# Second layer's weight split: the low part's tile starts from minus the raw tile instead of minus the high part

## The chip, the cores and the metric

The kernel runs on one NeuronCore of a Trainium2 chip. The metric is the device time of one execution in microseconds (us), the median over runs. Six names of engines occur: PE is TensorE (matrix products), ACT is ScalarE, DVE is VectorE, POOL is GpSimd, SP is SyncE, which here only issues transfers, and DMA is the transfer engines.

## The reference

One inference step of a decoder trunk of two layers, over 512 prompt tokens and 8 x 8 sample tokens (576 columns), model width 1024. The first layer is a gated linear recurrence (HGRN2); behind it one shared K/V is made, and the second layer is attention over a window of 128 positions with a sink per head, with 32 heads and an inner width of 2048:

```python
q, gate = swa_in(hp, w_in_b[j], norm_b[j])        # rms_norm(x) @ w_in, split into q and gate
hp = swa_out(hp, swa_prompt(q, kv_p, sinks_b[j]), gate, w_out_b[j])
...
def swa_out(x, o, gate, w_out):
    return x + (o.astype(F32) * jax.nn.silu(gate.astype(F32))).astype(x.dtype) @ w_out
...
y_prompt = rms_norm(hp, norm_f)
```

All of it is in fp32. Only the weights `w_in_b` (1024 x 4096) and `w_out_b` (2048 x 1024) of the second layer are touched by the change.

## The kernel before

PE takes its operands here in a rounded form of fp32 (fp32r). To keep the accuracy, each operand is split into a high part (the rounded value) and a low part (what the rounding left), and a product is made of three: high by high, high by low, low by high. `product_cols` issues them in just that order: first all `whi` by the high part of the data, then `whi` by its low part, and last `wlo` by the high part. So a weight's low part is wanted a good two thirds into its first product.

The weights come in blocks of 128 x 1024 through `split_weights`. SP issues the load of the raw block (L198), into one of three `raw` buffers. In the second layer (`share[0]` is None) the low part is not made by a subtraction on DVE or POOL, as in the first layer, but by a DMA: ACT casts the high part (L201), ACT writes minus the high part into the low tile (L202), and POOL issues a DMA that adds the raw block onto the low tile (L203). `whi` and `wlo` have two buffers each. A raw buffer is free again when its cast and its DMA are done, and only then can SP's next load into it start.

There are 48 such blocks: 16 `bq` (queries, `queries`), 16 `bg` (gates, `gates`), 14 `o` (output products, `out_halves`), and 2 last `o` blocks of `out_last`, whose parts are not `whi`/`wlo` but pieces of `xhi`/`xlo` (the split activations, no longer needed by then). The work is written as generators, and `merged` weaves the attention's steps with the parts of a string ORDER that ends in "q6 g6 q7 g7 O4 o6". Behind the last, `o6`, `out_last` makes the final product (`pz`), and then the final norm follows. The program is then scheduled by the framework: within an engine, instructions are put in an order by readiness and priority as it estimates them, and each engine works its own list in that order. So the order in the source isn't always the order on an engine.

Other names that occur below: `ohb`/`olb` are high and low parts of the gated attention output (cast at L1399 and L1271 on ACT, subtraction at L1400 on DVE), the data of the `po` products. `P`, `st`, `ph`, `pk`, `pav`, `low` belong to the attention's softmax and its product with V. `Qs` and `QS` are the queries, copied from the `pbq` products for sample and prompt tokens, and `scs` is the product of the sample queries with the cached keys.

Of the kernel before, what the change touches and what calls it, by code (L numbers as in the profile page):

```python
# [10 lines left out]
F32 = mybir.dt.float32  # L11
# [4 lines left out]
AF = mybir.ActivationFunctionType  # L16
ALU = mybir.AluOpType
# [66 lines left out]
def yoco_kernel(  # L84
# [26 lines left out]
    act, dve, pool, pe, sp = nc.scalar, nc.vector, nc.gpsimd, nc.tensor, nc.sync  # L111
# [83 lines left out]
    def split_weights(src, name, parts=None):  # L195
        n = src.shape[1] * src.shape[2]
        raw = wts.tile([P, 1024], F32, tag="raw", name=f"raw_{name}", bufs=3)
        sp.dma_start(raw[:, :n].rearrange("p (a c) -> p a c", a=src.shape[1]), src)  # L198
        hi, lo = parts or [wts.tile([P, 1024], F32R, tag=t, name=f"{t}_{name}") for t in ("whi", "wlo")]
        if share[0] is None:  # L200
            act.copy(hi[:, :n], raw[:, :n])  # L201
            act.activation(lo[:, :n], hi[:, :n].bitcast(F32), AF.Copy, scale=-1.0)  # L202
            pool.dma_start(lo[:, :n].bitcast(F32), raw[:, :n], accum_op=ALU.add)  # L203
            return hi, lo
        act.copy(hi[:, :n], raw[:, :n])  # L205
        c = n * share[0] // 8
        for eng, r in ((dve, slice(0, c)), (pool, slice(c, n))):
            if r.start < r.stop:
                eng.tensor_tensor(lo[:, r], raw[:, r], hi[:, r].bitcast(F32), ALU.subtract)  # L209
        return hi, lo  # L210
# [209 lines left out]
    def out_product(w_out, k0, ogs):  # L420

        nk = len(ogs)
        wd = 256 if nk > 2 else 512
        for mc in range(D // wd):
            src = w_out[0, k0 * P : (k0 + nk) * P, mc * wd : (mc + 1) * wd].rearrange("(k p) c -> p k c", p=P)
            whi, wlo = split_weights(src, f"o{k0}_{mc}")
            for c in range(wd // P):
                m = mc * (wd // P) + c
                pm = main(f"po{k0}_{m}")
                for _ in product(  # L430
                    pm,
                    whi,
                    wlo,
                    lambda k, j: ogs[k][0][:, j * HN : (j + 1) * HN],
                    lambda k, j: ogs[k][1][:, j * HN : (j + 1) * HN],
                    width=wd,
                    c0=c * P,
                    nk=nk,
                ):
                    pass  # L440
                h2 = s2(hT[:, m, :])
                with early():
                    dve.tensor_add(h2, h2, ps2(pm))  # L443
                yield

    def out_scaled(w_out, k0, ogs, gname, one):
# [4 lines left out]
        for mc in range(D // wd):  # L451
            src = w_out[0, k0 * P : (k0 + nk) * P, mc * wd : (mc + 1) * wd].rearrange("(k p) c -> p k c", p=P)
            whi, wlo = split_weights(src, f"o{k0}_{mc}")
            for c in range(wd // P):
                m = mc * (wd // P) + c
                pm = main(f"po{k0}_{m}")
                for _ in product(
                    pm,
                    whi,
                    wlo,  # L460
                    lambda k, j: ogs[k][0][:, j * HN : (j + 1) * HN],
                    lambda k, j: ogs[k][1][:, j * HN : (j + 1) * HN],
                    width=wd,
                    c0=c * P,
                    nk=nk,
                ):
                    pass
                h2 = hT[:, m, :]
                with tc.high_priority(offset=BOOST):
                    dve.tensor_add(s2(h2), s2(h2), ps2(pm))  # L470
                    act.activation(xhi[:, m, :], h2, AF.Copy, scale=vec(gname, m))
                    dve.scalar_tensor_tensor(
                        xlo[:, m, :], h2, vec(gname, m), xhi[:, m, :].bitcast(F32), ALU.mult, ALU.subtract
                    )
                    if m == 0:
                        act.activation(rall, h2, AF.Square)
                    else:
                        sq = one(f"nsq{m}")
                        act.activation(sq, h2, AF.Square)
                        (pool if m in SUM_POOL else dve).tensor_tensor(rall, rall, sq, ALU.add)  # L480

    def out_last(w_out, k0, ogs, each, between):


        nk = len(ogs)
        wd = 1024 // nk
        ws = []
        for mc in range(nk):
            src = w_out[0, k0 * P : (k0 + nk) * P, mc * wd : (mc + 1) * wd].rearrange("(k p) c -> p k c", p=P)
            parts = [view(x, [[1, 1024]], off=1024 * mc) for x in (xhi[:, 0, :], xlo[:, 0, :])]  # L490
            ws.append(split_weights(src, f"o{k0}_{mc}", parts))
        for j in range(2):
            for m in range(KT):
                pm = half(f"pz{k0}_{j}_{m}")
                product_half(pm, *ws[m * P // wd], lambda k: ogs[k], j, wd, m * P % wd, nk)
                h1 = hT[:, m, j * HN : (j + 1) * HN]
                with tc.high_priority(offset=BOOST):
                    dve.tensor_add(h1, h1, pm[:, :HN])
                    each(j, m)
                between(j, m)  # L500
# [30 lines left out]
    with ExitStack() as actx:  # L531
# [430 lines left out]
        for h in range(NH):  # L962
            nxt, chunks, n = {}, [], 0
# [21 lines left out]
    with ExitStack() as bctx:  # L985
# [34 lines left out]
        with tc.tile_pool(name="kvx", bufs=1) as kvx:  # L1020
# [24 lines left out]
            for c in range(4):  # L1045
# [17 lines left out]
                else:  # L1063
# [5 lines left out]
                    hi = Vc[:, :, g0 : g0 + 2, :64]  # L1069
# [508 lines left out]
```

## Time and profile before

| what | value |
|---|---|
| median of 3 runs | 1154.66 us (1153.55 to 1154.71) |
| profiled execution, its own time | 1152.44 us |
| its span in the trace | 1150.6 us |
| PE busy | 1105.9 us, 96% of the span |
| DVE busy | 857.6 us, 75% |
| ACT busy | 749.4 us, 65% |
| POOL busy | 265.9 us, 23% |
| mean granted clock of PE | 0.987 |

The span is the time from the first to the last instruction on the core; the profiled execution's own time holds 1.84 us beside it. All times of day below are microseconds from the start of the span. The second layer takes it from about 717 us on.

### The profile page before, as it was taken

What the parts mean: (1) busy time and instruction counts of PE and PEld (TensorE: products, weight loads), DVE (VectorE), ACT (ScalarE), POOL (GpSimd) and SP (SyncE); (2) the same over time, 40 slices, a digit from 0 to 9 for tenths busy, and PEclk for the clock granted to TensorE, in tenths of its full rate; (3) what the DMA queues carried; (4) which work ended last, traced back from release to release, by engine and by line L of the source; (5) the groups of instructions that cost most, each with busy time, mean ns of one, the idle gap of its engine ahead of it and who ended that gap; (6) DMA issues with size and microseconds to landing.
All of it is one profiled execution on the core that took longest, in us unless ns stands there. A gap on an engine that the chain in (4) does not pass through costs nothing.

```text
span 1150.6 us, 27472 instructions
## 1 busy us (share of the span) xinstructions
PE 1105.9 (96%) x10937; PEld 1072.6 (93%) x10937; DVE 857.6 (75%) x2090; ACT 749.4 (65%) x1748; POOL 265.9 (23%) x311
## 2 busy tenths in 40 slices
PE   5999999999999999999999989899999999999997
PEld 4999999998999899999999979899999998999996
DVE  8897777399985498875597887666676767576676
ACT  6677765367673467773566655678866876777665
POOL 1122221021221032121122143332332242232220
PEclk7999999999999999999999999999999999999998
DMA  5332333223233433323323223655545555554552
GB/s 157 93 113 78 104 94 113 77 79 108 71 118 107 122 87 110 89 76 107 96 71 110 86 77 92 143 137 117 132 114 126 129 128 134 126 127 113 127 111 83
DMA packets 168010, 123.19 MB, mean 107 GB/s; under 512 B 4665, under 2 KB 158314, under 8 KB 167850
## 3 DMA queue, kind: packets, MB, share of 16 engines
q1 hardware_dynamic: 160970, 96.26, 28.4%
q0 software_dynamic: 6912, 25.17, 11.6%
q8 instruction: 86, 1.41, 0.5%
q14 instruction: 42, 0.34, 0.1%
HBM read 84.06 MB, written 14.16 MB: 85 GB/s over the span
## 4 chain that ended last, share of the span: by engine, by line
PE 51%; DVE 6%; ACT 3%; issue 1%; DMA 1%; POOL 0%; DVEq 0%; POOLq 0%; ACTq 0%
PE pbg L216 8%; PE pbq L216 8%; PE po L216 6%; PE po L233 4%; PE pg L233 3%; PE pf L233 3%; PE pi L233 3%; PE pq L233 2%; PE sc L1103 2%; PE pkv L216 2%; PE pav L1186 1%; PE pz L216 1%; PE pa L802 1%; PE ptr L1154 1%; DMA wlo_o<-raw_o 1%
## 5 line engine op out<-in xcount | busy, mean ns | idle before, releaser
L205 ACT CAST whi_a<-raw_a 128x1024 fp32r<-128x1024 f32 x64 | 67.1, 1049 | 66.8 <-PE po L233 32.3
L209 DVE TENSOR_TENSOR wlo_a<-raw_a,whi_a 128x1024 fp32r<-128x1024 f32 x64 | 81.8, 1284 | 24.6 <-issue 23.2
L611 POOL TENSOR_TENSOR Xl<-Xl 128x72 f32<-128x72 f32 x80 | 49.6, 649 | 207.0 <-DVE Xl L608 205.7
L643 POOL TENSOR_TENSOR sg<-sg,lg 128x576 f32<-128x576 f32 x16 | 26.2, 1638 | 279.3 <-ACT lg L576 279.3
L1132 ACT ACTIVATE P<-P,st 128x192 f32<-128x192 f32 (+2 forms) x128 | 54.1, 424 | 38.4 <-DVE st L1127 38.3
L1141 POOL TENSOR_SCALAR P<-P,st 128x192 f32<-128x192 f32 (+1 forms) x64 | 47.9, 754 | 93.6 <-DVE st L1134 76.8
L443 DVE TENSOR_TENSOR hT<-hT,po 128x576 f32<-128x576 f32 x32 | 24.1, 754 | 51.0 <-PE po L233 50.7
L233 PE MATMUL po<-oh,whi_o 128*128 128x288 f32 x256 | 42.8, 302 | 4.4 <-ACT whi_o L205 1.9
L216 PE MATMUL po<-ohb,wlo_o 128*128 128x288 f32 x224 | 41.1, 297 | 2.2 <-DMA wlo_o<-raw_o 2.1
L667 POOL TENSOR_TENSOR vb<-vst,bmask 128x512 fp32r<-128x512 f32 x32 | 36.7, 1166 | 26.7 <-DVE vst L663 13.8
L216 PE MATMUL po<-ohb,whi_o 128*128 128x288 f32 x224 | 42.0, 302 | 0.2
L216 PE MATMUL pbq<-xhi,wlo_bq 128*128 128x256 f32 (+1 forms) x256 | 39.9, 297 | 2.4 <-DMA wlo_bq<-raw_bq 2.4
L233 PEld LDWEIGHTS po<-oh,whi_o 128*128 128x128 f32 x256 | 35.9, 188 | 6.4 <-ACT whi_o L205 2.2
L216 PE MATMUL po<-olb,whi_o 128*128 128x288 f32 x224 | 41.4, 298 | 0.5 <-DVE olb L1400 0.4
L233 PE MATMUL po<-ol,whi_o 128*128 128x288 f32 x256 | 41.4, 299 | 0.0
L233 PE MATMUL po<-oh,wlo_o 128*128 128x288 f32 x256 | 41.1, 298 | 0.0
L216 PE MATMUL pbq<-xhi,whi_bq 128*128 128x256 f32 (+1 forms) x256 | 40.5, 300 | 0.0
L216 PE MATMUL pbg<-xhi,whi_bg 128*128 128x288 f32 x256 | 40.5, 300 | 0.0
L216 PE MATMUL pbq<-xlo,whi_bq 128*128 128x256 f32 (+1 forms) x256 | 39.3, 296 | 0.0
L233 PE MATMUL pf<-xhi,wlo_a 128*128 128x288 f32 x256 | 37.5, 299 | 1.8 <-DVE wlo_a L209 1.8
L216 PE MATMUL pbg<-xhi,wlo_bg 128*128 128x288 f32 x256 | 39.1, 295 | 0.0
L233 PE MATMUL pf<-xhi,whi_a 128*128 128x288 f32 x256 | 39.1, 303 | 0.0
(390 smaller groups left out, 3676.7 us busy)
## 6 DMA issues: line engine op xcount, KB each, us to landing
raw_a<-in_w_in_a_dram SPq DMA_DIRECT2D x64, 512.0 KB
S<-in_state_hgrn_dram SPq DMA_DIRECT2D x32, 256.0 KB
out_dram<-S SPq DMA_DIRECT2D x32, 256.0 KB
raw_o<-in_w_out_a_dram SPq DMA_DIRECT2D x16, 512.0 KB
raw_bq<-in_w_in_b_dram SPq DMA_DIRECT2D x16, 512.0 KB
raw_bg<-in_w_in_b_dram SPq DMA_DIRECT2D x16, 512.0 KB
wlo_bq<-raw_bq POOLq DMA_DIRECT2D x16, 512.0 KB, 4.7
wlo_bg<-raw_bg POOLq DMA_DIRECT2D x16, 512.0 KB, 4.8
```

The costliest lines, as they stand in the source:

```text
L205: act.copy(hi[:, :n], raw[:, :n])
L209: eng.tensor_tensor(lo[:, r], raw[:, r], hi[:, r].bitcast(F32), ALU.subtract)
L216: pe.matmul(pm[:, : c1 - c0], w[:, k * width + w0 : k * width + w0 + P], x(k)[i][:, c0:c1], start=n == 0, stop=n == len(terms) - 1,)
L233: pe.matmul(pm[:, j, :HN], w[:, k * width + c0 : k * width + c0 + P], x(k, j), start=n == 0 and k == 0, stop=n == 2 and k == nk - 1,)
L443: dve.tensor_add(h2, h2, ps2(pm))
L611: pool.tensor_tensor(X8[:, :, j : j + 1], X8[:, :, j : j + 1], X8[:, :, k : k + 1], ALU.add)
L643: (pool if SGP else dve).tensor_tensor(sg, sg, l, ALU.mult)
L667: pool.tensor_tensor(t, view(vst.bitcast(F32), [[0, 4], [1, P]], off=half * P), view(bmask, [[1, 4], [0, P]]), ALU.mult,)
L802: pe.matmul(pa[32 * j : 32 * j + ns, c, t0 : t0 + nt], keys[:, c * P + s0 : c * P + s0 + ns], queries[:, c * P + t0 : c * P + t0 + nt], st ...
L1103: pe.matmul(sc[:, hf, k0[hf] :], QS[pr][:, 2 * n + hf, :], kk[:, g, ks], start=q == 0, stop=q == 1)
L1132: act.activation(x, x, AF.Exp, bias=st[:, a : a + 1], accum_out=st[:, 8 + a : 9 + a])
L1141: (pool if e == "p" else dve).tensor_scalar(x, x, st[:, 8 + a : 9 + a], None, ALU.mult)
```

## The change

Before, ACT cast the high part, then wrote minus the high part, read back from the high tile, and the DMA added the raw block. Now ACT writes minus the raw block, rounded to fp32r on the way, which is the same value; the DMA is issued behind that, and the cast of the high part stands last in the source. No instruction is added or removed, and the sizes are the same.

```diff
         if share[0] is None:
+            act.activation(lo[:, :n], raw[:, :n], AF.Copy, scale=-1.0)
+            pool.dma_start(lo[:, :n].bitcast(F32), raw[:, :n], accum_op=ALU.add)
             act.copy(hi[:, :n], raw[:, :n])
-            act.activation(lo[:, :n], hi[:, :n].bitcast(F32), AF.Copy, scale=-1.0)
-            pool.dma_start(lo[:, :n].bitcast(F32), raw[:, :n], accum_op=ALU.add)
             return hi, lo
```

The low part no longer reads the high tile, so the scheduler may place the two ACT instructions independently. In the changed program the cast is still the first of the two on ACT in 41 of the 48 blocks, at the place where it was, and the low part stays behind it where it was, but for two `bg` blocks in which it moves up directly behind the cast. In seven blocks the low part is first: three single ones (an `o` block each of O0 and of O2, and the last `bq` block), and the last four, near the end of the attention. SP issues the same transfers in the same order in both.

The last `bq` block, on ACT. This is the difference between the two lists (- before, + now); `wlo_bq_14069` and `whi_bq_14068` are the low and high part, `lb` belongs to the gates, `QS` is the queries' high part.

```order
 L1166 CAST pk_0_0_13938<-ptm_0_0_13929 64x256
 L1346 ACTIVATE lb_13923<-lb_13923 128x512
-L201 CAST whi_bq_14068<-raw_bq_14066 128x1024
+L201 ACTIVATE wlo_bq_14069<-raw_bq_14066 128x1024
 L1347 ACTIVATE lb_13923<-lb_13923 128x512
 L1291 CAST QS_0_13941<-pbq_0_13950 64x4x64 x2
-L202 ACTIVATE wlo_bq_14069<-whi_bq_14068 128x1024
+L203 CAST whi_bq_14068<-raw_bq_14066 128x1024
```

High and low part have changed places; nothing else moves here.

The end, on ACT, before. `raw_o_0_14931` and `raw_o_4_15019` are the two blocks of part `o6`; `raw_o_0_15118` and `raw_o_1_15123` are the two of `out_last`, in `xhi` and `xlo`.

```order
L201 CAST xhi<-raw_o_0_15118 128x1024
L201 CAST whi_o_0_14933<-raw_o_0_14931 128x1024
L1189 COPY low_1_0_14761<-pav_1_0_14757 64x512
L1256 COPY oS_14771<-pso_14226 64x256 x2
L1161 CAST ph_1_1_14782<-ptr_1_1_14774 128x512
L1166 CAST pk_1_1_14786<-ptm_1_1_14775 64x256 x2
L202 ACTIVATE wlo_o_0_14934<-whi_o_0_14933 128x1024
L202 ACTIVATE xlo<-xhi 128x1024
L201 CAST whi_o_4_15021<-raw_o_4_15019 128x1024
L1399 CAST ohb_0_14603<-sgt_13695 128x512
L1399 CAST ohb_1_14607<-sgt_13695 128x512
L1271 CAST ohb_0_14603<-oS_14771 128x64
```

And now:

```order
L201 ACTIVATE xlo<-raw_o_0_15118 128x1024
L201 ACTIVATE wlo_o_0_14934<-raw_o_0_14931 128x1024
L1189 COPY low_1_0_14761<-pav_1_0_14757 64x512
L1256 COPY oS_14771<-pso_14226 64x256 x2
L1161 CAST ph_1_1_14782<-ptr_1_1_14774 128x512
L1166 CAST pk_1_1_14786<-ptm_1_1_14775 64x256 x2
L203 CAST whi_o_0_14933<-raw_o_0_14931 128x1024
L203 CAST xhi<-raw_o_0_15118 128x1024
L201 ACTIVATE xlo<-raw_o_1_15123 128x1024
L1399 CAST ohb_0_14603<-sgt_13695 128x512
L1399 CAST ohb_1_14607<-sgt_13695 128x512
L1271 CAST ohb_0_14603<-oS_14771 128x64
```

Where the first two rows were casts, they are now low parts. Behind `pk` the list has the two casts (`whi_o_0`, `xhi`) where the two low parts were, and then `xlo<-raw_o_1_15123`, the low part of the program's last block, takes the place of the cast `whi_o_4` directly ahead of `ohb`. Before, that last block was first touched behind the next group's `ph` and `pk`, by its cast (`xhi<-raw_o_1_15123`).

The same end on POOL, with the semaphores that an instruction waits for (DMAHW4 is the load of `raw_o_0_15118`, DMAHW5 the load of `raw_o_1_15123`). Before:

```order
L1141 TENSOR_SCALAR P_1_2_14661<-P_1_2_14661,st_1_2_14662 128x192 [waits DVE_49,Activation_49,Pool_49]
L1141 TENSOR_SCALAR P_1_2_14661<-P_1_2_14661,st_1_2_14662 128x192 [waits Activation_49]
L203 DMA wlo_o_0_14934<-raw_o_0_14931 128x1024 [waits DMASW2_49,DMAHW2_49,PE_49,Activation_49]
L203 DMA xlo<-raw_o_0_15118 128x1024 [waits DMAHW4_49,Activation_49]
L203 DMA wlo_o_4_15022<-raw_o_4_15019 128x1024 [waits DMAHW3_49,DMASW3_49,Activation_49]
L1141 TENSOR_SCALAR P_1_3_14826<-P_1_3_14826,st_1_3_14827 128x192 [waits DVE_49,Activation_49,Pool_49]
L1141 TENSOR_SCALAR P_1_3_14826<-P_1_3_14826,st_1_3_14827 128x192 [waits Activation_49]
L203 DMA xlo<-raw_o_1_15123 128x1024 [waits DMAHW5_49,Activation_49]
```

And now:

```order
L1141 TENSOR_SCALAR P_1_2_14661<-P_1_2_14661,st_1_2_14662 128x192 [waits DVE_49,Activation_49,Pool_49]
L1141 TENSOR_SCALAR P_1_2_14661<-P_1_2_14661,st_1_2_14662 128x192 [waits Activation_49]
L202 DMA xlo<-raw_o_0_15118 128x1024 [waits DMAHW4_49,Activation_49]
L202 DMA wlo_o_0_14934<-raw_o_0_14931 128x1024 [waits DMAHW2_49,DMASW2_49,Activation_49]
L202 DMA xlo<-raw_o_1_15123 128x1024 [waits DMAHW5_49,Activation_49]
L202 DMA wlo_o_4_15022<-raw_o_4_15019 128x1024 [waits DMAHW3_49,DMASW3_49,Activation_49]
L1141 TENSOR_SCALAR P_1_3_14826<-P_1_3_14826,st_1_3_14827 128x192 [waits DVE_49,Activation_49,Pool_49]
L1141 TENSOR_SCALAR P_1_3_14826<-P_1_3_14826,st_1_3_14827 128x192 [waits Activation_49]
```

Each of the two `xlo` DMAs now stands ahead of one of `o6`'s.

SP's last loads of weights, before and now (the row of the last block is the one that differs):

```order
L198 DMA raw_o_6_14791<-in_w_out_b_dram 128x4x256 [waits DMAHW6_49,DMASW0_49,Activation_49]
L198 DMA raw_o_0_14931<-in_w_out_b_dram 128x2x512 [waits DMAHW7_49,DMASW1_49,Activation_49]
L198 DMA raw_o_4_15019<-in_w_out_b_dram 128x2x512 [waits DMAHW0_49,DMASW2_49,Activation_49]
L198 DMA raw_o_0_15118<-in_w_out_b_dram 128x2x512 [waits DMAHW1_49,DMASW3_49,Activation_49]
L198 DMA raw_o_1_15123<-in_w_out_b_dram 128x2x512 [waits DMAHW2_49,DMASW4_49,Activation_49]
```

```order
L198 DMA raw_o_6_14791<-in_w_out_b_dram 128x4x256 [waits DMAHW6_49,DMASW0_49,Activation_49]
L198 DMA raw_o_0_14931<-in_w_out_b_dram 128x2x512 [waits DMAHW7_49,DMASW1_49,Activation_49]
L198 DMA raw_o_4_15019<-in_w_out_b_dram 128x2x512 [waits DMAHW0_49,DMASW2_49,Activation_49]
L198 DMA raw_o_0_15118<-in_w_out_b_dram 128x2x512 [waits DMAHW1_49,DMASW3_49,Activation_49]
L198 DMA raw_o_1_15123<-in_w_out_b_dram 128x2x512 [waits DMAHW4_49,DMASW4_49,Activation_49]
```

The load of the last block `raw_o_1_15123` waited for the buffer of `raw_o_0_14931` (DMAHW2, the DMA DMASW4 of `wlo_o_0`). It now goes into the buffer of `raw_o_0_15118` (DMAHW4): it waits for that block's low part's DMA (DMASW4) and for its cast `xhi<-raw_o_0_15118` on ACT.

On PE the products are the same and in the same order, but for the attention's product `pav_1_2` near the end, whose first row stands three products further ahead between the `po` products, and whose later rows move by a few.

## Rows read from the trace of the kernel before

**Rows 1.** The page's first part: busy time of each engine, share of the span, instructions.

```profile
PE 1105.9 (96%) x10937; PEld 1072.6 (93%) x10937; DVE 857.6 (75%) x2090; ACT 749.4 (65%) x1748; POOL 265.9 (23%) x311
```

**Rows 2.** What PE waited for in the second layer: total us, times, longest.

```profile
PE pbq L216 <- DMA wlo_bq<-raw_bq: 2.4, 2, 1.4
PE po L216 <- DMA wlo_o<-raw_o: 2.1, 2, 1.7
```

**Rows 3.** Timeline of PE around 1050 us: start, us, instruction, [idle before <-releaser].

```profile
1044.56 0.86 PE L216 MATMUL pbq<-xhi,wlo_bq 128*128 128x256 f32 x5 [0.99 <-DMA wlo_bq<-raw_bq]
...
1055.83 0.45 PE L1210 MATMUL scs<-kcT,Qs 128*64 128x128 f32 x4 [1.12 <-DVE Qs L1299]
```

**Rows 4.** Timeline of ACT, POOL and DVE around the same places.

```profile
1035.95 1.04 ACT L201 CAST whi_bq<-raw_bq 128x1024 fp32r<-128x1024 f32 x1
...
1038.18 1.06 ACT L202 ACTIVATE wlo_bq<-whi_bq 128x1024 fp32r<-128x1024 f32 x1
...
1050.74 0.46 ACT L1132 ACTIVATE P<-P,st 128x192 f32<-128x192 f32 x1 [2.87 <-DVE st L1127]
...
1039.53 0.91 POOL L203 DMA_DIRECT2D wlo_bq<-raw_bq  x1 [0.62 <-PE pbq L216]
...
1055.31 0.46 DVE L1299 COPY Qs<-pbq 64x64 f32<-64x64 f32 x2
```

**Rows 5.** Timeline of ACT near the end of the attention, 1096 to 1113 us.

```profile
1096.24 1.05 ACT L201 CAST xhi<-raw_o 128x1024 fp32r<-128x1024 f32 x1 [1.99 <-DMA raw_o<-in_w_out_b_dram]
...
1100.88 1.06 ACT L202 ACTIVATE wlo_o<-whi_o 128x1024 fp32r<-128x1024 f32 x1
1101.85 1.04 ACT L202 ACTIVATE xlo<-xhi 128x1024 fp32r<-128x1024 f32 x1
1103.43 1.05 ACT L201 CAST whi_o<-raw_o 128x1024 fp32r<-128x1024 f32 x1 [0.54 <-PE po L216]
1104.39 1.14 ACT L1399 CAST ohb<-sgt 128x512 fp32r<-128x512 f32 x2
...
1112.00 1.05 ACT L201 CAST xhi<-raw_o 128x1024 fp32r<-128x1024 f32 x1 [1.33 <-DMA raw_o<-in_w_out_b_dram]
```

**Rows 6.** Timeline there of a DMA issue on POOL and of SP's loads.

```profile
1102.24 0.88 POOL L203 DMA_DIRECT2D wlo_o<-raw_o  x1 [5.86 <-ACT wlo_o L202]
...
1092.79 0.37 SPq L198 DMA_DIRECT2D raw_o<-in_w_out_b_dram  x1
...
1106.89 0.37 SPq L198 DMA_DIRECT2D raw_o<-in_w_out_b_dram  x1
```

**Rows 7.** Line L203: time from issue to landing of its DMAs.

```profile
DMA to landing us min/median/max: 4.5/5.0/7.4
```

**Rows 8.** Timeline of PE there, from the first product of the last o part.

```profile
1105.50 0.52 PE L216 MATMUL po<-ohb,whi_o 128*128 128x288 f32 x2
...
1106.39 0.40 PE L216 MATMUL po<-olb,whi_o 128*128 128x288 f32 x1 [0.20 <-DVE olb L1400]
...
1109.37 0.29 PE L216 MATMUL po<-ohb,wlo_o 128*128 128x288 f32 x1
1109.81 0.38 PE L1186 MATMUL pav<-ph,Vc 128*128 128x256 f32 x1
```

**Rows 9.** Timeline of PE behind three of its longer idle times.

```profile
382.06 0.79 PE L233 MATMUL po<-oh,whi_o 128*128 128x288 f32 x4 [1.93 <-ACT whi_o L205]
...
689.58 0.76 PE L1001 MATMUL pkc<-ident,ck 128*128 128x128 f32 x5 [1.94 <-DVE hT L470]
...
955.48 0.81 PE L216 MATMUL po<-ohb,wlo_o 128*128 128x288 f32 x4 [1.73 <-DMA wlo_o<-raw_o]
```

**Rows 10.** Windows behind them: PE, PEld, DVE, ACT, POOL busy, clock, DMA, GB/s.

```profile
383.30:386.60 3.30, 3.30 (x16) 3.30 (x15) 1.10 (x1) 0.00 (x0) 0.00 (x0) 0.50 0.66 189
690.50:693.80 3.30, 3.30 (x16) 3.30 (x15) 3.30 (x4) 0.70 (x2) 1.93 (x1) 0.50 0.53 140
955.50:958.80 3.30, 3.30 (x26) 3.30 (x27) 2.12 (x7) 3.00 (x5) 2.40 (x3) 1.00 0.48 159
```

## The prediction

> **What bounds the kernel now.** I read the page's busy times first: PE is busy for 1105.9 us, 96% of the span [rows 1], so the time changes only where PE's waits change, or its clock. Then the waits of PE in the second layer, which is the only part with changed weights: PE waits for the addition DMA of a low part four times, 2.4 us for `bq` and 2.1 us for `o` [rows 2], 4.5 us in all. This is all that an earlier low part could win there. Next, the timeline at two places, since the three lists of the change (ACT, POOL, SP) differ at few of the 48 blocks. The first is the last `bq` block, where PE waits 0.99 us for `wlo_bq` at 1044.56, and 10 us later 1.12 us for `Qs` from DVE at 1055.83 [rows 3]. The second is the end of the attention, where the last blocks of weights pass through ACT. There ACT's `ohb` at 1104.39 [rows 5] releases PE's first product of part `o6` at 1105.50, and PE meets the data just in time: it waits 0.20 us for `olb`, which is made from `ohb`, at 1106.39 [rows 8]. So whatever delays `ohb` on ACT delays PE by as much. ACT's idle share as a whole says nothing on this; the place does.
>
> **The swap itself.** Cast and negation take 1.04 and 1.06 us [rows 4], and each is still issued once, so ACT's work stays. In 41 blocks the cast is still first and the low part where it was, so the DMA is issued when it was. Three of the four waits in rows 2 belong to such blocks. I cost them at nothing; the low part no longer reads the cast's result, which could let the pair overlap by a few hundredths, as neighbours do (a start at 1101.85 while the one before, from 1100.88, ends at 1101.94 [rows 5]): 0.09 us in each of three waits, 0.3 us, is the bound of a gain.
>
> **The last `bq` block.** Here the low part takes the cast's place: 1035.95 in place of 1038.18 [rows 4], 2.2 us earlier. The DMA was issued at 1039.53, 0.29 us after the low part's end. It can now go out 2.2 us earlier, if nothing else holds it (POOL's row names PE as the releaser, so part of it may stay). PE's wait of 0.99 us then shrinks, to nothing at best. The cast comes 2.2 us later, from 1038.18 to about 1039.2; PE wants it 16 products, some 2.1 us, ahead of the wait that began at 1044.56 - 0.99 = 1043.57, so at about 1041.4, and nothing is late. But 11 us on, PE waits for `Qs`, 1.12 us [rows 3], and `Qs` on DVE (1055.31) stands behind a chain of attention steps on DVE and ACT (ACT's `P` at 1050.74 had itself waited 2.87 us for DVE's `st` [rows 4]) that doesn't pass through this DMA. PE arrives 0.99 us earlier and waits 0.99 us longer. So the gain goes from one wait into the next: 0, with 0.99 as the bound of what may survive if that chain moves along.
>
> **The end: the load of the last block.** This is the one large term, and it is a wait that is added. On ACT, `xlo<-raw_o_1_15123` now stands directly ahead of `ohb`, where the cast `whi_o_4` stood (1103.43). It needs the load of that block, and before, ACT came to that block only at 1112.00, having even there waited 1.33 us for the load [rows 5]. Step by step:
> - The first low part, `xlo` of `raw_o_0_15118`, stands where the cast stood: 1096.24 to 1097.29. POOL issued such a DMA 0.30 us after ACT's end (low part from 1100.88 for 1.06, issue at 1102.24 [rows 5, 6]), so now at 1097.6. It lands 4.5 to 7.4 us later, median 5.0 [rows 7]: at 1102.6, with 1105.0 as the late bound.
> - The cast `xhi` of that block now stands where `xlo` stood: 1101.85 to 1102.89 [rows 5]. With both done the buffer is free, and SP issues the last load at about 1102.95. Before, it was issued at 1106.89 [rows 6], so it is 3.9 us earlier, but ACT wants it 8.6 us earlier (1103.43 in place of 1112.00).
> - From issue to use a load took 3.45 us at the best (1092.79 to 1096.24, no addition DMA beside it) and 5.11 us (1106.89 to 1112.00, beside two of them) [rows 5, 6]. Now one addition, of `wlo_o_0`, issued right behind the first, is still on its way for the first 2 us or so; I take 3.8, nearer to the free case. ACT then starts `xlo` at 1106.75.
> - `ohb` follows 0.96 us behind (as 1104.39 behind 1103.43): 1107.7 in place of 1104.39, so 3.3 us late. The bounds: 2.9 with a free load, 4.6 with the slow one, 5.0 with a free load behind the late landing.
>
> What is queued behind that wait on ACT is `ohb`, then `wlo_o_4`, `low`, `P`, `ph` and `pk`, all moved as a block. PE stands at `po` from 1105.50 on with nothing else ahead of it in its own list, so the 3.3 us pass to it entirely. The cast `whi_o_4` moves behind `pk`, to about 1113.4; its products come behind eight sets of six, so not before 1115, and are not held up.
>
> **PE behind the stall.** The first row of `pav_1_2` stands three products earlier. PE already waited there: 1109.37 plus one product is 1109.50, the row started at 1109.81 [rows 8], so 0.3 us. Three products at 3.30 us / 26 = 0.127 us [rows 10] make 0.4 us more, if PE is at full clock. The clock may not be full: behind idle times of 1.93 and 1.94 us the granted clock was 0.50 in the next 3.3 us, behind one of 1.73 us it was 1.00 [rows 9, 10]. The stall is longer than all three, so I expect the fall. In such a stretch 16 products pass in place of 26: ten by 0.127 is 1.3 us. A slower PE arrives later at `pav`, so its wait there goes, the old 0.3 us too. With the fall the term is 1.3 - 0.3 = 1.0, without it 0.4.
>
> Beside this stands a rule: the Trainium skill, TensorE: Matmul & The Clock Gate, section HAM oscillation — how this bites in real kernels, describes products that wait for a transfer and whose next burst then runs at the halved clock every time, with half of the throttled time lost. By that rule the term would be 1.0 as well; the row at 955.48, a wait for a DMA with no fall behind it, disagrees with "every time" for a short one, and no row here has a stall of this length.
>
> **Sum.** 0 + 0 + 3.3 + 1.0 = +4.3 us. The profiled execution at 1152.44 us would go to 1156.7; the median lies 2.2 us above that execution, so 1154.66 + 4.3 = 1159.0.
>
> **The rivals.** A change within 0.2% (2.3 us) is about what a measurement of this kernel can't tell from none.
> - The stall without the clock's fall: 3.3 + 0.4 = 3.7, 1158.4. For it: the fall depends on more than the idle time's length, since 1.73 and 1.93 differ little and came out apart. Same side.
> - The load is slow or freed late (additions beside it): 4.6 to 5.0, plus 1.0: 5.6 to 6.0, 1160.3 to 1160.7. For it: 7.4 us in rows 7, and two additions go out in a row.
> - No stall: the last load is there before ACT comes to it. It decides at an issue by 1103.43 - 3.45 = 1099.98. Then all that's left is 0 to 0.99 at the `bq` block: 1153.7 to 1154.7. Against it: the cast that frees the buffer ends at 1102.89 at its place in ACT's list. For it: if ACT runs its list from 1098 to 1103 earlier, or a DMA lands faster than any in rows 7. The change would do next to nothing there.
> - The other side, faster: the negation without the cast ahead of it brings the DMA forward by a cast's 1.04 us at each of the four waits: 0.99 at one, and at the others, 4.5 - 0.99 = 3.5 us in three, up to 1.04 each, some 2.5. With no stall and no loss at `Qs` it is 3.5 us, 1151.2. It decides where the low part is first on ACT in those three blocks too. Against it: ACT's list there still has the cast first.
>
> **Chances.** Stall and fall 0.50; stall without fall 0.18; slow load 0.13; no stall 0.13; faster 0.06. A stall somewhat smaller than the bounds (a load faster than 3.45) without a fall would end near 2.3 us, which I count with the first two. So slower by over 0.2%: 0.80; within: 0.14; faster: 0.06. The range reaches from the free load without any loss of clock or at `pav` (2.9: 1157.6), less 0.8 for the spread of the runs shown, to the slow load with the fall and some spread: 1156.8 to 1161.2. It leaves out the no-stall cases, 0.19.
>
> **What would show it.** In the changed profile: ACT's `xlo<-raw_o` ahead of `ohb` with an idle time of 3 to 5 us ended by the load of `raw_o`; SP's last load near 1103; PE idle some 3 us at 1105.5 with ACT `ohb` or DVE `olb` as releaser, and a window behind it with a clock of 0.50 and 16 products; the wait at 1044.56 shorter and that for `Qs` longer by the same. It would be wrong if that load were issued before 1100, if the other three waits of rows 2 had moved, or if a later wait of PE took up the delay.

## The result and the profile after

The changed kernel takes 1156.84 us (median of 22 runs, 1154.23 to 1160.8), the kernel before 1153.45 (22 runs, 1151.3 to 1157.29): a ratio of 1.003 (95% interval 1.0022 to 1.0038), that is +3.4 us, with 2.5 to 4.4 by the interval. The forecast was +4.3 us, slower by more than 0.2%. The profiled execution took 1156.6 us, with a span of 1154.8 us; that of before 1152.44 and 1150.6, so between these two it is +4.2.

First what PE waited for in the second layer, after the change (total us, times, longest); it answers to [rows 2].

```profile
PE po L216 <- ACT ohb L1399: 2.7, 1, 2.7
PE po L216 <- DMA wlo_o<-raw_o: 2.4, 2, 1.5
PE scs L1210 <- DVE Qs L1299: 2.3, 2, 1.3
PE pbq L216 <- DMA wlo_bq<-raw_bq: 1.8, 2, 1.4
PE pbg L216 <- DMA wlo_bg<-raw_bg: 0.8, 1, 0.8
```

The first row is new, and with 2.7 us it is the largest wait of the layer. (The second wait for `wlo_bq` is a new one of 0.40 us at 732.76, and the shorter one for `wlo_o` has grown from 0.34 to 0.87 us, at 860.10; PE's rows before and after agree within 0.1 us again further on, 955.56 against 955.48 [rows 9].) Behind the first row stands the end of the attention, here in the timeline of ACT, with the issue on POOL and on SP; it answers to [rows 5, 6].

```profile
1096.22 1.06 ACT L201 ACTIVATE xlo<-raw_o 128x1024 fp32r<-128x1024 f32 x1 [1.98 <-DMA raw_o<-in_w_out_b_dram]
...
1100.89 1.05 ACT L203 CAST whi_o<-raw_o 128x1024 fp32r<-128x1024 f32 x1
1101.84 1.05 ACT L203 CAST xhi<-raw_o 128x1024 fp32r<-128x1024 f32 x1
1106.84 1.06 ACT L201 ACTIVATE xlo<-raw_o 128x1024 fp32r<-128x1024 f32 x1 [3.95 <-DMA raw_o<-in_w_out_b_dram]
1107.81 1.12 ACT L1399 CAST ohb<-sgt 128x512 fp32r<-128x512 f32 x2
...
1097.58 0.90 POOL L202 DMA_DIRECT2D xlo<-raw_o  x1 [1.20 <-ACT xlo L201]
...
1102.92 0.37 SPq L198 DMA_DIRECT2D raw_o<-in_w_out_b_dram  x1
```

The reader is to see four times: the first block's low part DMA is issued at 1097.58, the cast `xhi` ends at 1102.89, SP issues the last load at 1102.92, when its buffer is free, and ACT stands from 1102.89 to 1106.84, 3.95 us, until that load has landed. `ohb`, which needs nothing of it, comes behind it at 1107.81, 3.42 us later than before. PE there, answering to [rows 8]:

```profile
1108.46 0.92 PE L216 MATMUL po<-ohb,whi_o 128*128 128x288 f32 x2 [2.72 <-ACT ohb L1399]
...
1109.79 0.61 PE L216 MATMUL po<-olb,whi_o 128*128 128x288 f32 x1 [0.20 <-DVE olb L1400]
...
1113.59 0.28 PE L1186 MATMUL pav<-ph,Vc 128*128 128x256 f32 x1
```

The first product of `o6` starts at 1108.46 in place of 1105.50, and the second `olb` one at 1109.79 in place of 1106.39: 3.40 us later, the whole of ACT's delay. The row of `pav` has no wait any more. The chain of the work that ended last, over the same place (start, us, what), says it in one row: before, no transfer stood in it here.

```profile
1100.89 1.05 ACT whi_o L203
1101.94 0.97 ACT xhi L203
1102.92 3.90 DMA raw_o<-in_w_out_b_dram
1106.89 0.91 issue
1107.81 0.61 ACT ohb L1399
1108.44 1.31 DVE olb L1400 x2
1109.79 3.96 PE po L216 x17
```

Last the granted clock, in windows of PE behind the stall (columns as in [rows 10]):

```profile
1108.50:1109.30 0.80, 0.68 (x3) 0.45 (x3) 0.80 (x2) 0.80 (x4) 0.55 (x1) 1.00 0.00 0
1110.10:1110.90 0.80, 0.80 (x4) 0.80 (x4) 0.80 (x7) 0.80 (x3) 0.42 (x1) 0.50 0.87 169
1111.70:1112.50 0.80, 0.80 (x5) 0.80 (x5) 0.80 (x3) 0.80 (x4) 0.00 (x0) 0.50 0.92 164
1113.30:1114.10 0.80, 0.80 (x8) 0.80 (x7) 0.58 (x2) 0.76 (x3) 0.80 (x2) 1.00 1.20 225
```

It falls to 0.50 and is back at 1.00 by 1113.3: at 0.50 a window of 0.8 us holds 4 or 5 products, at 1.00 it holds 8, each time with those that only reach into it. At the next fixed point, ACT's `ohb` of the last pair, the delay has grown from 3.40 to 4.21 us, and so it stays to the end of the span, +4.2. The row before the change, and after it:

```profile
1121.88 1.14 ACT L1399 CAST ohb<-sgt 128x512 fp32r<-128x512 f32 x2 [2.11 <-DVE sgt L1197]
```

```profile
1126.09 1.14 ACT L1399 CAST ohb<-sgt 128x512 fp32r<-128x512 f32 x2 [2.12 <-DVE sgt L1197]
```

The other place of the forecast, the last `bq` block, answers to [rows 3]:

```profile
1052.59 1.19 PE L216 MATMUL pbg<-xhi,wlo_bg 128*128 128x288 f32 x7 [0.80 <-DMA wlo_bg<-raw_bg]
...
1055.83 0.45 PE L1210 MATMUL scs<-kcT,Qs 128*64 128x128 f32 x4 [1.27 <-DVE Qs L1299]
```

The wait of 0.99 us for `wlo_bq` at 1044.56 is gone. But PE now meets a wait of 0.80 us for `wlo_bg`, which it did not have before, and the wait for `Qs` is 1.27 us in place of 1.12. The product behind it starts at 1055.83, to the hundredth when it started before. The gain is given back in full within 12 us.

### The profile page after: what moved, and what is told of

It reads as the page before. It is cut to its first block, busy times and chain, and to the rows that moved or that the text cites. A ratio compares the mean times of both kernels' runs of the same rounds, so it can differ in the third digit from the quotient of the medians.

```text
span 1154.8 us, 27456 instructions
## 1 busy us (share of the span) xinstructions
PE 1105.8 (96%) x10937; PEld 1072.4 (93%) x10937; DVE 857.9 (74%) x2090; ACT 749.0 (65%) x1748; POOL 267.5 (23%) x311
## 3 DMA queue, kind: packets, MB, share of 16 engines
q8 instruction: 86, 1.41, 0.5%
## 4 chain that ended last, share of the span: by engine, by line
PE 45%; DVE 8%; ACT 6%; issue 2%; DMA 2%; POOL 1%; DVEq 0%; POOLq 0%; ACTq 0%
PE pbg L216 7%; PE po L216 6%; PE pbq L216 5%; PE po L233 4%; PE pg L233 3%; PE pf L233 3%; PE pi L233 3%; PE pq L233 2%; PE pkv L216 2%; ACT P L1132 2%; PE sc L1103 2%; PE pav L1186 1%; PE pz L216 1%; PE pa L802 1%; DMA wlo_o<-raw_o 1%
## 5 line engine op out<-in xcount | busy, mean ns | idle before, releaser
L205 ACT CAST whi_a<-raw_a 128x1024 fp32r<-128x1024 f32 x64 | 67.2, 1050 | 64.2 <-PE po L233 30.8
L1107 DVE CUSTOM_DVE_ANT_0 P<-sc,amask 128x192 f32<-128x192 f32 (+2 forms) x128 | 36.4, 329 | 3.7 <-PE sc L1103 3.2
```

Source lines behind the costliest of these rows:

```text
L1107: dve.tensor_tensor_reduce(Pt[:, pr, hf, k0[hf] :], sc[:, hf, k0[hf] :], amask[:, k0[hf] :], 0.125, NEG, ALU.add, ALU.max, accum_out=st[:, ...
```

## Experiments

The theory: all of the loss is ACT's place. The last block's first instruction stands ahead of `ohb`, ACT works its list in order, and the block's load can't be there. The rivals: the other moved low parts cost something, or the order on ACT costs it whatever the load does.

**The last block behind ohb (c_behind_ohb).** The whole change stays; the scheduler is told to queue the last block's ACT instructions behind `ohb`.

```diff
-                act.copy(oh[:, :LP], sgt[:, pr, :])
+                ohb[i] = act.copy(oh[:, :LP], sgt[:, pr, :])
...
-            ws.append(split_weights(src, f"o{k0}_{mc}", parts))
+            with tc.issue_after(ohb[6].ins) if mc else ExitStack(): ws.append(split_weights(src, f"o{k0}_{mc}", parts))
```

> The change as it is, and only ACT's instructions for the very last block are queued behind the cast ohb of the last o part; ACT's list then differs from that of the changed kernel by 15 lines, all at this place, and PE's list is that of before. Theory 1 (all of the loss is ACT standing at the last load with ohb behind it): ohb starts at 1104.4 us again, PE's wait of 2.7 us for ohb is gone, and the time is that of before within 0.1%, so some 3.4 us below the changed kernel. Theory 2 (the loss comes from the low parts and DMAs that moved elsewhere, such as PE's new wait of 0.8 us for wlo_bg): PE's wait for ohb may go, but 1 to 3 us over before are left.

Measured: 1152.57 us against 1153.24 for before on the same chip, ratio 0.9993 (0.9983 to 1.0004): no difference to before. Timelines of ACT and PE at the end, and of PE at the earlier place:

```profile
1104.54 1.14 ACT L1399 CAST ohb<-sgt 128x512 fp32r<-128x512 f32 x2
...
1106.54 0.40 PE L216 MATMUL po<-olb,whi_o 128*128 128x288 f32 x1 [0.20 <-DVE olb L1400]
...
1052.68 1.19 PE L216 MATMUL pbg<-xhi,wlo_bg 128*128 128x288 f32 x7 [0.80 <-DMA wlo_bg<-raw_bg]
...
1055.92 0.45 PE L1210 MATMUL scs<-kcT,Qs 128*64 128x128 f32 x4 [1.26 <-DVE Qs L1299]
```

`ohb` is at 1104.54 and PE waits only the old 0.20 us for `olb`, while the wait for `wlo_bg` (0.80) is still there. So the loss is this one place on ACT, and the moved low parts elsewhere cost nothing that this measurement can tell (it reaches from 2.0 us below before to 0.5 above); nor do they bring anything. One thing goes with the place: PE's list is that of before in this run, so `pav_1_2` stands where it stood, too. What its earlier place costs by itself, 0.4 us by the prediction, no run shows alone.

**A buffer of its own for the last load (d_own_buffer).** The order on ACT keeps the last block ahead of `ohb`; what its load waits for is taken away. (The scheduler then puts the block's cast and `whi_o_4` ahead of `ohb` too.)

```diff
-        raw = wts.tile([P, 1024], F32, tag="raw", name=f"raw_{name}", bufs=3)
+        raw = per.tile([P, DB, P], F32, tag="cv", name=f"raw_{name}", bufs=1).rearrange("p a b -> p (a b)") if parts and name.endswith("_1") else wts.tile([P, 1024], F32, tag="raw", name=f"raw_{name}", bufs=3)
```

> The change as it is, but the last block is loaded into a tile of its own (that of the cached values, free once PE's last pso product is done, near 1096.5 us), so its load does not wait for the cast and the DMA of the block before it. ACT's list has the low part, the cast of the last block and the cast whi_o_4 ahead of ohb. Theory 1 (the load that comes late is what ACT stands at): the load is issued near 1097 and is there before 1102.9, ACT does not idle ahead of it, ohb starts after the two further instructions at 1104.4 + 1.9 - 0.5 = 1105.8, PE idles 1.4 us there with no fall of the clock, and the time is 1.0 to 1.6 us above before. Theory 2 (ACT's order alone costs it, whatever the load does): the loss stays at 3.4 us or more.

Measured: 1153.78 us against 1153.24, ratio 1.0008 (0.9996 to 1.002): +0.9 us, not clear of nothing (-0.5 to 2.3), and less than the change's loss (2.5 to 4.4). The load was now issued at 1096.34. Its timeline, ACT and then PE, and two windows behind it:

```profile
1102.91 1.05 ACT L201 ACTIVATE xlo<-raw_o 128x1024 fp32r<-128x1024 f32 x1
...
1105.75 1.13 ACT L1399 CAST ohb<-sgt 128x512 fp32r<-128x512 f32 x2
...
1107.74 0.40 PE L216 MATMUL po<-olb,whi_o 128*128 128x288 f32 x1 [0.20 <-DVE olb L1400]
```

```profile
1105.50:1108.80 3.30, 2.44 (x14) 1.74 (x13) 2.40 (x11) 3.30 (x8) 0.37 (x1) 1.00 0.84 159
1108.80:1112.10 3.30, 2.90 (x22) 2.67 (x22) 3.21 (x9) 3.17 (x13) 0.49 (x1) 1.00 0.73 139
```

ACT goes from the cast straight into the last block without idle time, `ohb` starts at 1105.75 (1105.8 was expected), PE's product at 1107.74 is 1.35 us later than before, and the clock stays at 1.00. By these rows the order alone costs the two further instructions that went ahead; the rest was the load.

**The change without the last product's two blocks, and in these alone (e1_all_but_last, e2_last_only).** The first keeps the old lines for the blocks of `out_last`:

```diff
         if share[0] is None:
+            if parts:
+                act.copy(hi[:, :n], raw[:, :n])
+                act.activation(lo[:, :n], hi[:, :n].bitcast(F32), AF.Copy, scale=-1.0)
+                pool.dma_start(lo[:, :n].bitcast(F32), raw[:, :n], accum_op=ALU.add)
+                return hi, lo
             act.activation(lo[:, :n], raw[:, :n], AF.Copy, scale=-1.0)
```

and the second has `if not parts:` there.

> The change in all blocks but the two of the last product, which keep the cast first. ACT's list still has the last block's first instruction (here its cast) directly ahead of ohb, and its load takes the buffer of the block before, behind the DMA of wlo_o_0. Theory 1: that DMA is issued near 1098.5 and lands near 1103, the load is issued then, beside the DMA of the first xlo, so it takes nearer 5 than 3.5 us; ohb some 4 to 4.6 us late; with the fall of the clock 5 us over before. Rival (the swap within the last pair makes the loss): 0 over before.

> The change in the two blocks of the last product alone. Theory 1: the load is issued near 1103 as in the changed kernel, but the DMA of wlo_o_0 goes out at 1102.2 and lies beside it all the time, so the load takes nearer 5 than 3.9 us; ohb some 4 to 4.6 us late, 5 us over before. Theory 2 (the loss comes from the other 46 blocks): 0 over before. With e1_all_but_last at 5 as well, either part alone is enough to bring the last block ahead of ohb.

Measured: 1159.44 and 1159.48 us against 1153.24, ratios 1.0057 (1.0038 to 1.0075) and 1.0052 (1.0035 to 1.0068): 6.2 us over before each by the medians, 4 to 8.6 by the intervals; the expected 5 lies inside. For each, first the timeline, SP's load, ACT at the last block and PE at `o6`, then a window behind the stall; e1_all_but_last, with PE's row at `pz` as well:

```profile
1103.16 0.37 SPq L198 DMA_DIRECT2D raw_o<-in_w_out_b_dram  x1
...
1107.22 1.04 ACT L202 CAST xhi<-raw_o 128x1024 fp32r<-128x1024 f32 x1 [4.29 <-DMA raw_o<-in_w_out_b_dram]
...
1108.84 0.92 PE L221 MATMUL po<-ohb,whi_o 128*128 128x288 f32 x2 [3.08 <-ACT ohb L1404]
...
1128.14 1.05 PE L221 MATMUL pz<-ohb,xhi 128*128 128x288 f32 x5 [1.19 <-ACT ohb L1404]
```

```profile
1112.10:1115.40 3.30, 3.30 (x19) 3.30 (x18) 2.39 (x8) 3.24 (x12) 1.44 (x2) 0.64 0.84 159
```

And e2_last_only, with POOL's issue ahead of the load:

```profile
1102.95 0.86 POOL L204 DMA_DIRECT2D wlo_o<-raw_o  x1 [3.77 <-PE po L221]
...
1103.61 0.37 SPq L198 DMA_DIRECT2D raw_o<-in_w_out_b_dram  x1
...
1109.49 1.06 ACT L206 ACTIVATE xlo<-raw_o 128x1024 fp32r<-128x1024 f32 x1 [5.90 <-DMA raw_o<-in_w_out_b_dram]
...
1111.11 1.13 PE L221 MATMUL po<-ohb,whi_o 128*128 128x288 f32 x2 [4.78 <-ACT ohb L1404]
```

```profile
1112.10:1115.40 3.30, 3.30 (x14) 3.00 (x14) 3.25 (x15) 3.27 (x12) 0.00 (x0) 0.50 0.84 159
```

Either part of the change alone brings the last block ahead of `ohb` (in e1 by its cast), and either stalls more than the whole change: ACT waits 4.29 and 5.90 us, PE 3.08 and 4.78 us. The longer wait is that in which `wlo_o_0`'s DMA goes out with the load. The clock falls behind both. In e1 the time was as expected, the way only in part: the load took 4.06 us from issue to use and not nearer 5, `ohb` came 3.8 us late (1108.17) and not 4 to 4.6, and PE's stall is only 0.4 us longer than the change's 2.72. A further 1.0 us lies at `pz`, where PE waits 1.19 us for the last `ohb` and waited 0.2 us before; f_lo_first, below, has the same wait. In e2 the load took 5.9 us, and `ohb` came some 5.4 us late (1110.45, less 0.7 us by which this execution already stood behind at 1096 us), more than the 4 to 4.6 expected. E1's profiled execution was the shortest of its six, so its rows show less than its median.

**The low part first everywhere (f_lo_first, f_o_first).** On top of c_behind_ohb, the cast of each block is queued behind its low part; in f_o_first only in the `o` blocks.

```diff
-            act.activation(lo[:, :n], raw[:, :n], AF.Copy, scale=-1.0)
+            first = act.activation(lo[:, :n], raw[:, :n], AF.Copy, scale=-1.0)
             pool.dma_start(lo[:, :n].bitcast(F32), raw[:, :n], accum_op=ALU.add)
-            act.copy(hi[:, :n], raw[:, :n])
+            with tc.issue_after(first.ins): act.copy(hi[:, :n], raw[:, :n])
```

> As c_behind_ohb (the last block behind ohb), and in every one of the 48 blocks the cast is queued behind the low part, which is what the source order of the change says but the scheduler does in seven blocks only. Reading of the diff (the rival that I gave the faster side): the low parts' DMAs go out 1 to 4 us earlier, PE's four waits for them, 4.5 us in all, shrink to 1 us or less, and the time is 3 us or more below before. Theory: the waits shrink in the rows, but PE then waits for the next thing, attention steps of DVE and ACT as at 1055 us, and for casts that now come later; 0 to 1.5 us below before.

> As f_lo_first, but only in the blocks of the output products is the cast queued behind the low part; the others stay as in c_behind_ohb. Two of PE's four waits (2.1 us) are for these. Reading of the diff: they go, 1.5 to 2 us below before. Theory: the one at 955 us, where the low part stood 3.7 us behind its cast, shrinks; what is left of it behind the next wait is 0 to 1 us, so 0 to 1 us below before.

Measured: f_lo_first 1150.58 us against 1152.37, ratio 0.9985 (0.9975 to 0.9994), by it 1.7 us below before; f_o_first 1153.21, ratio 1.0001 (0.9991 to 1.0012), no difference. Waits of PE in f_lo_first over the second layer:

```profile
PE pvw L1067 <- DVE kf L1035: 2.5, 2, 1.4
PE pz L216 <- ACT ohb L1399: 1.2, 1, 1.2
PE pav L1186 <- ACT ph L1161: 1.0, 1, 1.0
PE po L216 <- DMA wlo_o<-raw_o: 0.6, 1, 0.6
PE pbq L216 <- DMA wlo_bq<-raw_bq: 0.3, 1, 0.3
```

The four waits for the additions are down from 4.5 us to 0.9. Of these 3.6 us, 1.1 came back at once as a second wait for `kf` in `pvw` (2.5 in two, 1.4 in one before), and at the end two waits have grown, to 1.0 for `ph` and 1.2 for `ohb` in `pz`, from 0.3 [rows 8] and 0.2 before. The result lies a little beyond the theory's 1.5 and well short of the reading's 3. In f_o_first the wait near 955 us was still 1.48 us (1.41 in c_behind_ohb), though its DMA went out at 947.48 in place of 950.80. Of these 3.3 us, 2.4 are no gain: PE, too, stands that much earlier in this execution (the last `pbq` products ahead of it start at 940.30 and 942.70). The other 0.9 us went into the addition itself, from whose issue to PE's product 5.71 us passed in place of 4.86; why stays open. Its end, moreover, has the same two waits as f_lo_first, 1.0 and 1.2 us.

**The low part first, but the end as before (g_first_but_end).**

```diff
-            with tc.issue_after(first.ins): act.copy(hi[:, :n], raw[:, :n])
+            with ExitStack() if name[:3] in ("o12", "o14") else tc.issue_after(first.ins): act.copy(hi[:, :n], raw[:, :n])
```

> As f_lo_first (low part ahead of the cast), but the four blocks at the end (part o6 and the last product) are as in c_behind_ohb. In f_lo_first the stretch up to 1101 us ran 2.8 us ahead of before (ohb at 1101.61 in place of 1104.39), and the end gave 1.7 us of it back, in PE's waits of 1.0 us for ph and 1.2 us for ohb, with ACT's list changed there. Theory (the end's order is what gave it back): both waits go back to 0.4 and 0.2 us, 2.5 to 3.5 us below before. Rival (PE has only arrived earlier at chains that end when they did): the waits stay, 1.5 us below before as f_lo_first.

Measured: 1149.94 us against 1153.21, ratio 0.9975 (0.9963 to 0.9987): by it 2.9 us below before (1.5 to 4.3), and 0.55% below the changed kernel, from the two ratios to before. PE at the end, in f_lo_first and then in g_first_but_end:

```profile
1107.94 0.38 PE L1186 MATMUL pav<-ph,Vc 128*128 128x256 f32 x1 [0.96 <-ACT ph L1161]
...
1121.51 1.05 PE L216 MATMUL pz<-ohb,xhi 128*128 128x288 f32 x5 [1.18 <-ACT ohb L1399]
```

```profile
1107.62 0.39 PE L1186 MATMUL pav<-ph,Vc 128*128 128x256 f32 x1 [0.40 <-ACT ph L1161]
...
1120.37 1.18 PE L216 MATMUL pz<-ohb,xhi 128*128 128x288 f32 x6 [0.21 <-ACT ohb L1399]
```

The two waits are back at 0.4 and 0.2 us, as the theory had it. The rows carry this: by the time alone, 1.5 to 4.3 us, the rival's 1.5 isn't clearly out, nor is g_first_but_end clearly faster than f_lo_first. What differs in ACT's list can be named. Between the `ohb` casts of `o6` and the `low` behind them, f_lo_first, f_o_first and e1_all_but_last have two weight instructions of 1 us (`wlo_o_4` and the cast `whi_o_4`), all the other kernels one, and `pz` waits 1.2 us in those three and 0.2 us in all the others. No run moves that cast alone. By their ratios to before, this version beats both kernels. One caution on single profiles: executions already differ by a microsecond ahead of any changed instruction (f_lo_first has PE's row of 689.58 [rows 9] at 688.30), so the 2.8 us that I read in f_lo_first at 1101 us may hold up to 1.3 us of that. Such an offset needn't last: the changed kernel's rows stood 0.5 us ahead of before's at 721 us and level with them at 800. So its own gain there was between 1.5 and 2.8 us.

## Why the prediction was right

- **The swap itself, 0.** Right: c_behind_ohb holds all of it but the one place, and stands at 0.9993. The sign of being wrong that I gave, the other three waits moving, did show in a small way (1.40 to 1.36, 0.34 to 0.87, 1.73 to 1.49 us, and a new one of 0.40); it left no difference by 955 us.
- **The last `bq` block, 0.** Right in the sum, only partly in the way. The wait of 0.99 us went, as said, and PE's product behind `Qs` started at 1055.83 as before. But I had the whole of it go into the wait for `Qs`; in fact 0.80 us went into a wait for `wlo_bg`, whose DMA comes when it always came, and 0.15 us into that for `Qs`.
- **The load of the last block.** Each step came out close: issue at 1102.92 (1102.95), load 3.92 us to its use (3.8), `xlo` at 1106.84 (1106.75), `ohb` at 1107.81 (1107.7), PE's delay 3.40 us (3.3). That it is the wait for the load, held by the buffer, is shown by c_behind_ohb (order undone) and d_own_buffer (load freed) together. (The prediction's bound of 2.9 us for a free load is 3.0 by its own terms.)
- **PE behind the stall, 1.0.** The clock fell to 0.50, the wait at `pav` went, and the net was 4.21 - 3.40 = 0.8 us. That the clock would fall rested on the length of the stall against 1.93 and 1.73 us, and that is weaker than I took it to be. The same wait of 1.93 us that brought a fall to 0.50 before [rows 9, 10] stands in the changed kernel's profile at 382.84, with no fall behind it:

```profile
384.30:387.60 3.30, 3.30 (x27) 3.30 (x27) 1.64 (x2) 0.00 (x0) 0.00 (x0) 1.00 0.64 185
```

So a wait of that length brings the fall in one execution and not in another. Behind the stalls of 2.72, 3.08 and 4.78 us the clock fell in all three profiles; for the executions that were not profiled no row shows it.

- **Sum.** +4.3 forecast, +4.2 between the two profiled executions, +3.4 between the medians (2.5 to 4.4). The 0.8 us between the last two I can't place; the profiled executions stand 1.0 us below (before) and 0.2 us below (after) their medians. My 1159.0 was taken from a median of three runs that was itself 1.2 us above the median of 22. With that the measured 1156.84 fell on the very edge of my range, which begins at 1156.8: the mechanism was right, but that the time lies inside is luck by a few hundredths of a microsecond.
- **The rivals.** That there would be no stall failed, since the load was issued at 1102.92 and not by 1099.98. The slow load did not come in this kernel (3.92 us) nor in e1_all_but_last (4.06), but did in e2_last_only (5.9). The faster side needed the low part first in most blocks; forced, it was worth 1.7 us (0.7 to 2.9), and 2.9 us (1.5 to 4.3) with the end kept, an interval that holds the rival's 3.5 us.
- **The skill's rule on the clock.** The Trainium skill, TensorE: Matmul & The Clock Gate, section HAM oscillation — how this bites in real kernels, describes a kernel in which PE waits some 3 to 5 us for each transfer, and every burst behind such a wait runs at the halved clock. Here the stall ahead of 1108.46 was followed by windows at 0.50, and so were those of e1_all_but_last and e2_last_only; that agrees, though with 2.72 us the first is a little shorter. The prediction held the row at 955.48 [rows 9] against the page, but the page doesn't say this of a wait of 1.73 us.

## What to carry to other kernels

When a dependency is taken away, look at the order in which each engine then works, not at the diff: here the scheduler kept the cast first in 41 of 48 blocks, and its one harmful move was an instruction whose load had not landed, put ahead of work that had nothing to do with it. Price such a move as the time when the load's buffer is free, plus the load, minus when the engine comes there, and give all of it to whatever stands behind on that engine. And of a wait that shrinks in the middle of a chain, count nothing until you have named the next wait of the same engine.

## What I had not expected of the hardware

Where the addition DMA of one block and a load went out nearly together (e2_last_only: issues at 1102.95 and 1103.61), ACT waited for that load until 1109.49, 5.9 us after its issue; in the changed kernel, with the last addition issued 4.4 us ahead of the load, 3.92 us. I had taken 5.11 us [rows 5, 6] for the slow end.

The times of issue alone don't tell a slow load from a fast one: in e1_all_but_last an addition went out at 1103.22, 0.06 us behind the load, which took 4.06 us. The packets recorded in the traces do. In the changed kernel the additions' packets had all started before the load's first, and the load's 256 packets took 1.95 us. In e1_all_but_last an addition's packets fell on the last 0.6 us of the load's 2.7. In e2_last_only they fell on the first 2.3 us of the load's 3.5: in that time 8 to 30 of its packets started in half a microsecond, and 95 and 76 in the two that followed. So a load whose packets meet an addition's can take 2 us longer than one whose packets don't, and no wait in the trace names that: it shows only as a later landing.
